# Spare bytes put the operands of all products at the same place modulo 512 bytes, and the software DMA scratch is halved

## The chip, the cores and the metric

The kernel runs on one core of one Trainium2 chip. Time is device time in microseconds (us) of one execution, the median of the runs shown; smaller is better. The engines are TensorE (PE, with its weight loads as PEld), VectorE (DVE), ScalarE (ACT), GpSimd (POOL) and SyncE (SP).

## The reference, cut to what matters

Two layers of a streaming encoder for 256 tokens of width 2048, all in float32. In each layer:

```
h = rms_norm(x, pre_mix_norm);  proj = h @ w_in                  # u, c_kv|k_pe, c_q, gate logits
a = mla(c_q, c_kv, k_pe) @ w_o                                   # 16 heads, chunk-causal mask
s = GLU(gelu(S5 scan of u) @ w_glu)
m = sigmoid(g_a) * a + sigmoid(g_b) * s
x = x + rms_norm(m @ w_out, post_mix_norm)
h = rms_norm(x, pre_ffn_norm)
x = x + rms_norm((silu(h @ w_gate) * (h @ w_up)) @ w_down, post_ffn_norm)
```

## The kernel before

All large products go through `gemm` (line 413). A weight matrix is taken in pieces of 256 rows by 512 columns. SP fetches a piece into a `raw` tile, ACT rounds it to float32r into a `hi` tile (line 187), and DVE subtracts the two into a `lo` tile (line 151, through the `Counted` wrapper). The activations lie split in the same way, feature by feature, as high and low parts. A product of 128 tokens, 128 features and 512 columns is then three matmuls, lines 444 to 446: high part with `hi`, high part with `lo`, low part with `hi`. In each of them the weights (`hi`, `lo`) are the moving operand, 512 columns of 4 bytes, so 2048 bytes of each partition, and the activations are the stationary operand, 128 columns of 4 bytes, so 512 bytes of each partition. A weight load (PEld) precedes each matmul, since the stationary operand alternates.

The stationary operand is, by stage: tile `H` for u, c_kv|k_pe, c_q, the gates, w_o and the gate and up products of the feed-forward; `uz` for w_glu; `mT` for w_out; `aT` for w_down. The c_kv|k_pe product alone has 320 columns in place of 512.

In the attention (lines 1293 to 1356) it is the other way round: the weight parts are stationary, and the activations `cqT` (lines 1306 to 1308) and `ckvT` (lines 1333 to 1335) move, 256 columns at a time; the values (lines 1351 to 1353) have the weights moving again. The S5 part has float32r products `bu` of `uz` with `bd` (lines 991 to 993). Transposes (line 467), scores, the products with the probabilities and `y` (line 1001) are plain float32. All these are set between or beside the large products by a planner in Python (`Background`), which fixes each engine's order when the program is built.

| tile | starts at | modulo 512 |
|---|---|---|
| `cs` (the identity among it) | 16512 | 128 |
| `raw`, `hi`, `lo` (15 tiles of 4096 bytes) | 17568 and on | 160 |
| `H` | 79008 | 160 |
| `X` (tokens by features, also the attention's arena) | 111776 | 160 |
| `uz`, and `aT` in its room later | 134880 | 224 |
| `mT` | 151264 | 224 |
| S5 tiles (`E`, `P`, `bd`, `xx`), layer 0, layer 1 | 163840 to 197120 | 0, 352 |
| `cqT`, layer 0, layer 1 | 203264, 202592 | 0, 352 |
| `ckvT`, `kpeT`, `pT`, layer 0, layer 1 | 198496 to 223743 | 0, 352 |

Inside a tile all the operands of 512 columns, 256 columns and 128 columns start at multiples of 512 bytes. The one exception is the second half of a weight piece in the 320-column product, which starts 1280 bytes into its tile, so at 416 modulo 512.

At the end of a mix or a feed-forward, `boundary` (line 669) adds the residual: POOL loads it in chunks `xo` and writes the new x (lines 684 and 690), DVE adds.

## Time and profile before

| | |
|---|---|
| median of 3 runs (lowest, highest) | 2937.29 us (2936.51, 2938.09) |
| span of the profiled execution | 2934.7 us |
| PE busy | 2902.1 us, 99% of the span |
| PEld, DVE, ACT busy | 80%, 65%, 48% |
| POOL busy | 33.1 us, 1% |
| HBM traffic | 188 GB/s over the span |

The span runs from the first to the last instruction; the profiled execution's time is not given apart, so 2937.29 - 2934.7 = 2.6 us are taken as lying around the span. PE's busy time is no measure of its pace, since matmuls overlap and their ends are modelled: two matmuls that start 227 ns apart both show some 390 ns. The pace is read from the starts.

### The profile page before, as it was taken

To read this page: it belongs to the slowest core of one execution; us is meant where nothing else is said; L and a number is where in the kernel's file an instruction comes from. 1 tells how busy PE (TensorE), PEld (TensorE's weight loads), DVE (VectorE), ACT (ScalarE), POOL (GpSimd) and SP (SyncE) were. 2 spreads that over 40 slices of the span, in tenths; PEclk is the share of its full clock that TensorE was granted. 3 is DMA by queue.
4 is the path that set the end of the run, shared out by engine and by line. 5 is a ranking of instruction groups with operands and counts; after the bars stand their busy time and mean duration, and the time that the engine had idled before them with its cause. 6 is when DMAs were issued, how large, how long until landed. Compare 5 with 4: busy or idle time off the path is not lost.

```text
span 2934.7 us, 37400 instructions
## 1 busy us (share of the span) xinstructions
PE 2902.1 (99%) x13557; PEld 2350.9 (80%) x13557; DVE 1902.7 (65%) x2988; ACT 1413.1 (48%) x2343; POOL 33.1 (1%) x65
## 2 busy tenths in 40 slices
PE   8999999999999999999999999999999999999998
PEld 7777887787788888888877778878878888888887
DVE  7888998765765554544478888986665554454444
ACT  6655665444544444333366556644445444444333
POOL 0000000000000000000000000000000000000000
PEclk9999999999999999999999999999999999999999
DMA  7666335666666666655576663357666566666554
GB/s 220 200 197 185 110 117 180 210 214 202 216 204 202 188 192 193 189 192 192 173 228 195 193 187 112 116 182 240 214 205 206 180 193 195 185 187 229 190 192 142
DMA packets 311222, 553.77 MB, mean 189 GB/s; under 512 B 44353, under 2 KB 57085, under 8 KB 310653
## 3 DMA queue, kind: packets, MB, share of 16 engines
q1 hardware_dynamic: 301708, 528.43, 57.8%
q0 software_dynamic: 4544, 14.42, 1.5%
q10 hardware_dynamic: 4784, 8.53, 0.8%
q8 instruction: 106, 1.74, 0.2%
q14 instruction: 80, 0.65, 0.1%
HBM read 532.74 MB, written 18.56 MB: 188 GB/s over the span
## 4 chain that ended last, share of the span: by engine, by line
PE 96%; DVE 2%; DMA 1%; ACT 0%; issue 0%; SPq 0%; DVEq 0%; ACTq 0%
PE acc L444 28%; PE acc L446 28%; PE acc L445 28%; PE y L1001 2%; PE aux L467 2%; PE bu L991 1%; PE acc L1306 1%; PE acc L1308 1%; PE acc L1307 1%; DVE lo L151 1%; PE bu L992 1%; PE bu L993 1%; PE aux L1286 0%; PE aux L1237 0%; PE aux L1238 0%
## 5 line engine op out<-in xcount | busy, mean ns | idle before, releaser
L151 DVE TENSOR_TENSOR lo<-raw,hi 128x1024 fp32r<-128x1024 f32 (+3 forms) x992 | 1147.8, 1172 | 620.9 <-PE acc L445 413.4
L187 ACT ACTIVATE hi<-raw 128x1024 fp32r<-128x1024 f32 (+3 forms) x992 | 994.1, 1018 | 748.6 <-PE acc L446 573.7
L444 PE MATMUL acc<-hi,H 128*128 128x512 f32 (+1 forms) x2432 | 963.7, 396 | 0.4 <-ACT X L264 0.3
L446 PE MATMUL acc<-hi,H 128*128 128x512 f32 (+1 forms) x2432 | 945.0, 389 | 4.6 <-DVE H L151 4.6
L445 PE MATMUL acc<-lo,H 128*128 128x512 f32 (+1 forms) x2432 | 944.4, 388 | 1.2 <-DVE lo L151 1.2
L444 PEld LDWEIGHTS acc<-hi,H 128*128 128x128 f32 x2432 | 457.2, 188 | 108.2 <-issue 13.2
L446 PEld LDWEIGHTS acc<-hi,H 128*128 128x128 f32 x2432 | 457.0, 188 | 103.5 <-DVE H L151 8.8
L445 PEld LDWEIGHTS acc<-lo,H 128*128 128x128 f32 x2432 | 457.7, 188 | 90.0 <-DVE lo L151 2.6
L444 PE MATMUL acc<-hi,aT 128*128 128x512 f32 x704 | 278.7, 396 | 0.0
L445 PE MATMUL acc<-lo,aT 128*128 128x512 f32 x704 | 278.4, 395 | 0.0
L446 PE MATMUL acc<-hi,aT 128*128 128x512 f32 x704 | 278.4, 395 | 0.0
L446 PEld LDWEIGHTS acc<-hi,aT 128*128 128x128 f32 x704 | 132.3, 188 | 32.0
L444 PEld LDWEIGHTS acc<-hi,aT 128*128 128x128 f32 x704 | 132.4, 188 | 31.8
L445 PEld LDWEIGHTS acc<-lo,aT 128*128 128x128 f32 x704 | 132.4, 188 | 31.8
L444 PE MATMUL acc<-hi,uz 128*128 128x512 f32 x256 | 102.4, 400 | 1.6 <-ACT uz L264 1.6
L444 PE MATMUL acc<-hi,mT 128*128 128x512 f32 x256 | 101.4, 396 | 0.0
L446 PE MATMUL acc<-hi,uz 128*128 128x512 f32 x256 | 101.2, 395 | 0.0
L445 PE MATMUL acc<-lo,uz 128*128 128x512 f32 x256 | 101.2, 395 | 0.0
L446 PE MATMUL acc<-hi,mT 128*128 128x512 f32 x256 | 100.9, 394 | 0.0
L445 PE MATMUL acc<-lo,mT 128*128 128x512 f32 x256 | 100.9, 394 | 0.0
L264 ACT ACTIVATE X<-acc,rstd 128x512 f32<-128x512 f32 (+1 forms) x64 | 41.2, 651 | 121.0 <-PE acc L446 119.4
L264 ACT ACTIVATE aT<-aux 128x512 fp32r<-128x512 f32 x44 | 26.1, 598 | 146.2 <-PE aux L467 146.2
(194 smaller groups left out, 2702.8 us busy)
## 6 DMA issues: line engine op xcount, KB each, us to landing
raw<-in_w_in_dram SPq DMA_DIRECT2D x176, 512.0 KB, 4.3
raw<-in_w_ffn_gate_dram SPq DMA_DIRECT2D x176, 512.0 KB, 4.2
raw<-in_w_ffn_up_dram SPq DMA_DIRECT2D x176, 512.0 KB, 3.8
raw<-in_w_ffn_down_dram SPq DMA_DIRECT2D x176, 512.0 KB, 4.4
raw<-in_w_o_mla_dram SPq DMA_DIRECT2D x64, 512.0 KB, 4.0
raw<-in_w_glu_dram SPq DMA_DIRECT2D x64, 512.0 KB, 4.9
raw<-in_w_out_dram SPq DMA_DIRECT2D x64, 512.0 KB, 4.7
raw<-in_w_uq_dram SPq DMA_DIRECT2D x32, 384.0 KB, 3.6
```

Source lines behind the costliest of these rows:

```text
L151: return f(**kw)
L187: self.nc.scalar.activation(out=dst(hv), in_=src(self.raw[n]), func=AF.Copy)
L264: ACT.activation(out=o, in_=x, func=f, **kw)
L444: PE.matmul(out=o, lhsT=xh, rhs=h[:, kk], start=(k == 0), stop=False)
L445: PE.matmul(out=o, lhsT=xh, rhs=lo[:, kk], start=False, stop=False)
L446: PE.matmul(out=o, lhsT=xl, rhs=h[:, kk], start=False, stop=(k == nk - 1))
L467: PE.transpose(o, x, ident[0:rows, 0:rows])
L991: PE.matmul(out=o, lhsT=bd[r, 0, i], rhs=uh, start=True, stop=False)
L992: PE.matmul(out=o, lhsT=bd[r, 1, i], rhs=uh, start=False, stop=False)
L993: PE.matmul(out=o, lhsT=bd[r, 0, i], rhs=ul, start=False, stop=True)
L1001: PE.matmul(out=yo, lhsT=cm[:, i, c].rearrange("p g q -> p (g q)"), rhs=xx[:, i], start=(i == 0), stop=(i == 1))
L1306: PE.matmul(out=o, lhsT=hi, rhs=cqT[:, 0, k], start=(k == 0), stop=False)
```

## The change

A helper `spare` takes a named tile that nothing reads or writes. It is called in three pools, so that what follows lies further up: 352 bytes behind `cs`, 448 bytes behind the tile `zero`, and 224 (layer 0) or 384 (layer 1) bytes at the head of the S5 pool. The scratch of the software DMAs goes from 16384 to 8192 bytes, which makes room for them. The rest of the diff blanks comments. On every engine the instructions, their order, their shapes and their waits are the same as before; only the addresses differ.

```diff
+    def spare(pool, n):
+
+        T(pool, [128, n // 4], "spare")
+
...
     cs = T(cp, [128, 262], "cs")
     ACT.dma_start(out=cs, in_=cst)
+    spare(cp, 352)
...
     zero = T(vp, [128, 1], "zero")
+    spare(vp, 448)
     V.memset(ap=zero, constant=0.0)
...
         def s5(l=l, gains=gains):
+            spare(sp, 224 if l == 0 else 384)
             tab = T(sp, [128, 928], "seeds")
...
-    nc = _bacc.Bacc("TRN2", target_bir_lowering=False, num_devices=1)
+    nc = _bacc.Bacc("TRN2", target_bir_lowering=False, num_devices=1, dynamic_dma_scratch_size=8192)
```

In the changed program `raw`, `hi`, `lo`, `H`, `X`, `uz`, `aT`, `mT`, `cqT`, `ckvT`, `kpeT`, `pT`, `bd` and `xx` all start at 0 modulo 512, in both layers. `cs` stays at 128, and the second half of a piece in the 320-column product lies at 256. `H` starts at byte 71168, `uz` and `aT` at 127488, `mT` at 143872.

## Rows read from the trace of the kernel before

**Rows 1.** The page: busy times, and the chain that ended last.

```profile
PE 2902.1 (99%) x13557; PEld 2350.9 (80%) x13557; DVE 1902.7 (65%) x2988; ACT 1413.1 (48%) x2343; POOL 33.1 (1%) x65
...
PE 96%; DVE 2%; DMA 1%; ACT 0%; issue 0%; SPq 0%; DVEq 0%; ACTq 0%
```

**Rows 2.** PE's groups by line and shape: count | busy us, mean ns | idle before.

```profile
L444 PE MATMUL acc<-hi,H 128*128 128x512 f32 x2368 | 943.2, 398 | 0.1
...
L444 PE MATMUL acc<-hi,aT 128*128 128x512 f32 x704 | 278.7, 396 | 0.0
...
L444 PE MATMUL acc<-hi,uz 128*128 128x512 f32 x256 | 102.4, 400 | 1.6 <-ACT uz L264 1.6
L444 PE MATMUL acc<-hi,mT 128*128 128x512 f32 x256 | 101.4, 396 | 0.0
...
L1306 PE MATMUL acc<-cqT,hi 128*128 128x256 f32 x192 | 58.0, 302 | 0.0
...
L991 PE MATMUL bu<-uz,bd 32*128 32x256 f32 x128 | 42.1, 329 | 0.0
...
L1333 PE MATMUL acc<-ckvT,hi 128*128 128x256 f32 x64 | 20.9, 326 | 0.0
...
L1351 PE MATMUL acc<-hi,ckvT 128*128 128x256 f32 x64 | 19.2, 300 | 0.0
```

**Rows 3.** Stretches with H, aT, mT, uz: length; busy us by engine; PEclk, DMA share.

```profile
975.00:1000.00 25.00, 25.00 (x112) 20.71 (x111) 13.16 (x12) 10.70 (x11) 0.00 (x0) 1.00 0.55 168
1230.00:1430.00 200.00, 200.00 (x859) 161.12 (x858) 91.93 (x82) 79.13 (x84) 0.00 (x0) 1.00 0.58 193
650.00:675.00 25.00, 25.00 (x109) 20.03 (x108) 11.24 (x11) 9.40 (x12) 0.00 (x0) 1.00 0.59 201
555.00:562.00 7.00, 7.00 (x31) 5.64 (x30) 6.30 (x8) 3.48 (x4) 0.00 (x0) 1.00 0.35 109
```

**Rows 4.** PE's timeline (start us, us): first and last matmul with H, and with aT.

```profile
974.66 0.39 PE L444 MATMUL acc<-hi,H 128*128 128x512 f32 x1
...
999.82 0.39 PE L444 MATMUL acc<-hi,H 128*128 128x512 f32 x1
...
1229.80 0.40 PE L446 MATMUL acc<-hi,aT 128*128 128x512 f32 x1
...
1429.99 0.40 PE L446 MATMUL acc<-hi,aT 128*128 128x512 f32 x1
```

**Rows 5.** PE's timeline, layer 0: y, then second and last of 24 q products.

```profile
343.31 1.05 PE L1001 MATMUL y<-xx,cm 128*32 128x256 f32 x4
...
344.51 0.28 PE L1307 MATMUL acc<-cqT,lo 128*128 128x256 f32 x1
...
347.14 0.29 PE L1308 MATMUL acc<-cqT,hi 128*128 128x256 f32 x1
```

**Rows 6.** Layer 1: y, then second, seventh and last of 24 q products.

```profile
1802.28 1.05 PE L1001 MATMUL y<-xx,cm 128*32 128x256 f32 x4 [0.40 <-DVE xx L151]
...
1811.94 0.28 PE L1307 MATMUL acc<-cqT,lo 128*128 128x256 f32 x1
...
1812.53 0.28 PE L1306 MATMUL acc<-cqT,hi 128*128 128x256 f32 x1
...
1814.46 0.28 PE L1308 MATMUL acc<-cqT,hi 128*128 128x256 f32 x1
```

**Rows 7.** PE's timeline, the 320-column product: first and last of 15.

```profile
61.78 0.31 PE L444 MATMUL acc<-hi,H 128*128 128x320 f32 x1
...
63.83 0.31 PE L446 MATMUL acc<-hi,H 128*128 128x320 f32 x1
```

**Rows 8.** DVE's groups, 60 to 420 us (layer 0), then 1530 to 1880 us (layer 1).

```profile
L151 DVE TENSOR_TENSOR P<-E,Z 128x512 f32<-128x512 f32 x47 | 31.4, 709 | 0.0
...
L151 DVE TENSOR_TENSOR P<-E,Z 128x512 f32<-128x512 f32 x52 | 34.6, 707 | 0.0
```

**Rows 9.** The chain of waits at the first boundary: start us, us, what.

```profile
727.32 5.78 DMA xo<-in_x_dram
```

## The prediction, made before the changed kernel ran

> **What bounds the kernel now.** I read the page first: PE is busy for 99% of the span, and the chain that ended last is 96% PE [rows 1]. PE's groups show next to no idle time before the large products, 0.0 to 1.6 us in a whole group [rows 2]. So no wait is left to remove. What can change is the pace at which PE goes through its matmuls, and that is all an address can touch here. The next view is therefore the start times.

> In a stretch with one stationary tile, the count of the stretch less one, over the time from its first to its last start, is the pace. With H: (999.82 - 974.66) / 111 = 226.7 ns. With aT: (1429.99 - 1229.80) / 858 = 233.3 ns. mT and uz are read from the counts of their stretches, which take in the matmul that reaches over the stretch's start: with a length of 0.39 us each, 25.00 us show (25.00 + 0.39) / 0.2267 = 112.0 at H's pace and 108.8 at aT's. H shows 112, mT 109. 7.00 us show 32 or 33 at H's pace and 31 or 32 at aT's; uz shows 31. So both go at aT's pace [rows 3, 4]. [...] Rows, columns and type are the same in all four. What differs is the place: with H moving and stationary operand both lie at 160 modulo 512, with the other three the moving one lies at 160 and the stationary one at 224.

> Layer 0 and layer 1 are a second pair, with the same code: the 24 q products have the moving cqT at 0 and at 352, the stationary weights at 160 in both. From the second to the last, 22 steps: 2.63 / 22 = 119.5 ns in layer 0 and 2.52 / 22 = 114.5 ns in layer 1, and its last 17 steps go at (1814.46 - 1812.53) / 17 = 113.5 ns [rows 5, 6]. So the place does act on float32r products, and by some 7 ns of each.

> **The change part by part.** No instruction is added, removed or moved, so each term is a count by a change of pace.

> *aT, uz, mT: from (160, 224) to (0, 0).* The lines 444, 445 and 446 have equal counts; with aT 3 x 704 = 2112 matmuls, with uz and with mT 3 x 256 = 768 each, in all 3648 [rows 2]. If what counts is that both operands lie at the same place, they take H's pace: 233.3 - 226.7 = 6.67 ns each (13.3 against 20.0 ns over the columns), so 3648 x 6.67 ns = 24.3 us less. All of it lies on PE, so on the path. Could something else become late there? At H's pace a stage already gets its weights: 12 matmuls eat a piece in 2.72 us, with DVE 13.2 of 25 us busy and ACT 10.7, and the DMA engines at a share of 0.55. With aT DVE is 91.9 of 200 us busy, ACT 79.1, the DMA share 0.58 [rows 3]. 3% more pace raises them by 3%. The cover stays.

> *H: from (160, 160) to (0, 0).* 3 x 2368 = 7104 matmuls of 512 columns [rows 2]. No row has two operands of such a product at 0. [...] I take no change, by the nearest row: in the 320-column product the moving operand lies at 160 for three matmuls and at 416 for the next three, with H at 160 in both, and the 15 go evenly, 2.05 / 14 = 146.4 ns or 13 ns over the 133.3 ns of the columns, as with H everywhere [rows 7]. A shift by 256 bytes does nothing, so a start on the 512-byte boundary is nothing special by itself, and the fine grid has to be below 256 bytes.

> [...]

> *256-column products: to (0, 0).* Each of these groups has three lines of equal count: q 3 x 192 = 576, half of them in each layer, keys 3 x 64, values 3 x 64, bu 3 x 128, in all 1344 [rows 2]. If the 13.3 ns of H hold for them too, they go at 106.7 + 13.3 = 120.0 ns. Layer 1's q then lose (120.0 - 114.5) x 288 = 1.6 us, layer 0's 0.1 us; the other 768 I leave where they are. The two paces seen, 113.5 and 119.5 ns, bound them: all at the one or all at the other moves 768 by at most 6 ns either way, 4.6 us, and with the q's a bound of 6 us either way. I take 1.7 us more.

> *Plain float32 products.* Four products of y take 1.05 us in layer 0 (xx at 0) and 1.05 us in layer 1 (xx at 352) [rows 5, 6]. They do not feel the place. I take nothing for them, nor for the scores and transposes, which have no such pair of rows.

> *DVE and ACT.* In S5 DVE's P<-E,Z took 709 ns with its tiles at 0 and 707 ns with them at 352 [rows 8]. raw, hi and lo keep their places to each other. Nothing. If it were something, PE would cover it in most stages, since DVE is busy for 65% [rows 1].

> *The halved scratch.* It concerns POOL's DMAs. POOL is busy for 33.1 us of the span in all [rows 1], so there are few of them. But the residual's load is on the chain at a boundary, 5.78 us [rows 9], so a delay there would count. I take nothing; if each of the loads that the chain waits for came one landing (5.78 us) later, three boundaries would cost 17 us.

> *The sum:* -24.3 + 1.7 = -22.6 us. From the span, 2934.7 - 22.6 = 2912.1, and with the 2.6 us around it 2914.7 us, against the median of 2937.29.

> **The rivals.**

> *The place is not the cause.* H lies in the lower part of the partition (from byte 79008), aT, uz and mT above 134880, and they stay up there. If the height makes the 6.67 ns, nothing changes: 2937. For it: in the large products height and place go together. Against it: cqT lies at 203264 and 202592 in the two layers, the same height, and its pace differs; and aT reaches over 90 KB without a change of pace over 200 us. [...]

> [...]

> *Slower: 0 is a bad place for H.* If the common place counts too and 0 costs what 224 does, H goes to 233.3 ns, +47.4 us, and the rest gains nothing: 2985. It decides from 22.6 us / 7104 = 3.2 ns per product with H; above that the gain is eaten. For it: the moving cqT at 0 is the slower of the two layers [rows 5, 6]. Against: there the stationary operand lies at 160, so that the two differ by 160, not by 0.

> *The scratch bites:* 2914.7 + 17 = 2932.

> **How the numbers follow.** A difference of 0.2%, 5.9 us, is about what a measurement can tell from no change. Forecast 66% (own range 2908 to 2922, from the 6 us of the 256-column products); place not the cause 10%; H gains too 12%, wholly or in part; H loses 10%; the scratch 2%. The range takes in the unchanged time above, and of the case in which H gains the part up to about half its gain: 2885 to 2939. Faster: 66 + 12 = 78%; same: 10 + 2 = 12%; slower: 10%.

> **What would show it.** The stretches with aT, uz and mT at 226.7 ns between starts, H's still at 226.7, the 320-column product at 146.7; q at 120 in both layers; P<-E,Z at 708 ns; the residual's loads landing in some 5 us as now. Wrong if aT stays at 233.3 ns (height), or if H's pace moves at all: 7104 matmuls make 7.1 us of each nanosecond.

## The result, and the profile after

The changed kernel takes 2914.05 us (median of 4 runs, 2913.07 to 2915.5) against 2937.11 us before (4 runs, 2936.51 to 2938.09): a ratio of 0.9921 with a 95% interval of 0.9907 to 0.9936. It is faster by 23.1 us, 0.8%. The forecast was 2914.7 us.

The page after: the span, PE's and the other engines' busy time, and the chain that ended last.

```profile
span 2913.7 us, 37400 instructions
...
PE 2882.4 (99%) x13557; PEld 2353.5 (81%) x13557; DVE 1902.1 (65%) x2988; ACT 1412.6 (48%) x2343; POOL 33.1 (1%) x65
...
PE 96%; DVE 2%; DMA 1%; ACT 1%; issue 0%; DVEq 0%; ACTq 0%
```

Against [rows 1] the counts are the same on every engine, PE is as full as it was and the chain is still 96% PE. DVE and ACT work as long as before. PE's idle time, span less busy, goes from 2934.7 - 2902.1 = 32.6 us to 2913.7 - 2882.4 = 31.3 us. So nearly all of the gain is not a wait: the same matmuls follow one another more closely. Of PE's waits the one for `bx` in S5 moved most, before and after (us in total, times, longest):

```profile
PE y L467 <- ACT bx L264: 1.6, 1, 1.6
...
PE y L472 <- ACT bx L268: 0.3, 1, 0.3
```

In the other profiled executions below this wait is between 0.0 and 2.1 us, wherever the tiles lie, so the change can't be credited with it.

Lines of the kernel stand 4 to 7 further down than before: 448 to 450 are the three products of `gemm`, 1313 to 1315 those of q.

The same four stretches as in [rows 3] (H, aT, mT, uz), 5 to 10 us earlier since the work ahead is done sooner: length; busy us of PE, PEld, DVE, ACT, POOL; clock, DMA share, GB/s.

```profile
965.00:990.00 25.00, 25.00 (x112) 20.72 (x111) 11.45 (x10) 10.98 (x12) 0.00 (x0) 1.00 0.65 197
1222.00:1422.00 200.00, 200.00 (x884) 165.66 (x883) 95.13 (x85) 81.58 (x87) 0.00 (x0) 1.00 0.61 200
645.00:670.00 25.00, 25.00 (x112) 20.69 (x111) 12.65 (x12) 10.01 (x13) 0.00 (x0) 1.00 0.62 212
549.00:556.00 7.00, 7.00 (x32) 5.77 (x32) 1.32 (x3) 1.99 (x3) 0.40 (x1) 1.00 0.52 168
```

H shows 112 matmuls in 25 us, as before. aT shows 884 in 200 us in place of 859, mT 112 in place of 109, uz 32 in place of 31. For uz 32 fits either pace in so short a stretch; what decides is the mean over its products that follow one another directly, 227.1 to 227.6 ns in the two layers where it was 233.3. The clock is 1.00 in both kernels, so it is not the clock. The weights keep up: DVE's share with aT goes from 91.9 to 95.1 us of 200, ACT's from 79.1 to 81.6.

PE's timeline (start us, us), the first and last matmul of the stretch with H and of the one with aT:

```profile
964.70 0.39 PE L449 MATMUL acc<-lo,H 128*128 128x512 f32 x1
...
989.86 0.39 PE L449 MATMUL acc<-lo,H 128*128 128x512 f32 x1
...
1221.78 0.39 PE L448 MATMUL acc<-hi,aT 128*128 128x512 f32 x1
...
1421.93 0.39 PE L449 MATMUL acc<-lo,aT 128*128 128x512 f32 x1
```

H: (989.86 - 964.70) / 111 = 226.7 ns, as in [rows 4]. aT: (1421.93 - 1221.78) / 883 = 226.7 ns, where [rows 4] had 233.3.

The q products after, second and last of 24, in layer 0 and then in layer 1, with a y product of layer 1 (lines 1313 to 1315 and 1008):

```profile
343.72 0.28 PE L1314 MATMUL acc<-cqT,lo 128*128 128x256 f32 x1
...
346.34 0.28 PE L1315 MATMUL acc<-cqT,hi 128*128 128x256 f32 x1
...
1786.70 0.28 PE L1314 MATMUL acc<-cqT,lo 128*128 128x256 f32 x1
...
1789.33 0.28 PE L1315 MATMUL acc<-cqT,hi 128*128 128x256 f32 x1
...
1791.81 1.05 PE L1008 MATMUL y<-xx,cm 128*32 128x256 f32 x4 [0.34 <-DVE xx L151]
```

Layer 0 goes at 2.62 / 22 = 119.1 ns, as it did [rows 5]. Layer 1 goes at 2.63 / 22 = 119.5 ns where it had 114.5 [rows 6]: it lost 5 ns a product. y is as it was.

The 320-column product in PE's timeline, first and last of 18:

```profile
60.52 0.30 PE L448 MATMUL acc<-hi,H 128*128 128x320 f32 x1
...
63.01 0.31 PE L450 MATMUL acc<-hi,H 128*128 128x320 f32 x1
```

DVE's groups in layer 1 (count | busy us, mean ns | idle before):

```profile
L151 DVE TENSOR_TENSOR P<-E,Z 128x512 f32<-128x512 f32 x50 | 33.3, 709 | 0.0
```

The residual's load on the chain at the first boundary (start us, us, what):

```profile
723.26 5.32 DMA xo<-in_x_dram
```

2.49 / 17 = 146.5 ns per product, 709 ns (706 in layer 0), 5.32 us: all three as before [rows 7 to 9].

**Where the 21.0 us of the span went.** I added up the distances from each matmul's start to the next one's, over both whole traces, by group (us):

| group | before | after | difference |
|---|---|---|---|
| aT | 492.9 | 478.9 | -14.0 |
| mT | 179.7 | 174.8 | -4.9 |
| uz | 182.3 | 178.5 | -3.9 |
| H, 512 columns | 1655.7 | 1657.2 | +1.6 |
| q | 72.8 | 73.8 | +1.1 |
| keys and values | 51.4 | 51.7 | +0.3 |
| transposes of X | 50.3 | 51.2 | +0.9 |
| transposes of `bx` | 5.2 | 3.8 | -1.4 |
| ahead of the first matmul | 5.8 | 5.4 | -0.5 |
| all of the span | 2934.7 | 2913.7 | -21.0 |

What is left, some 0.3 us, is spread over groups that each move by 0.2 us or less.

### The profile page after: what moved, and what is told of

Same layout as the page of the kernel before. It is cut to its first block, busy times and chain, and to the rows that moved or that the text cites. A ratio compares the mean times of both kernels' runs of the same rounds, so it can differ in the third digit from the quotient of the medians.

```text
span 2913.7 us, 37400 instructions
## 1 busy us (share of the span) xinstructions
PE 2882.4 (99%) x13557; PEld 2353.5 (81%) x13557; DVE 1902.1 (65%) x2988; ACT 1412.6 (48%) x2343; POOL 33.1 (1%) x65
## 4 chain that ended last, share of the span: by engine, by line
PE 96%; DVE 2%; DMA 1%; ACT 1%; issue 0%; DVEq 0%; ACTq 0%
PE acc L448 28%; PE acc L449 28%; PE acc L450 28%; PE y L1008 2%; PE aux L472 2%; PE bu L998 1%; PE acc L1313 1%; PE acc L1314 1%; PE acc L1315 1%; DVE lo L151 1%; DMA xo<-x 1%; PE bu L999 1%; DVE X L151 1%; PE bu L1000 1%; PE aux L1293 1%; PE aux L1244 0%
## 5 line engine op out<-in xcount | busy, mean ns | idle before, releaser
L448 PEld LDWEIGHTS acc<-hi,H 128*128 128x128 f32 x2432 | 457.5, 188 | 108.9 <-issue 13.2
L448 PE MATMUL acc<-hi,aT 128*128 128x512 f32 x704 | 274.4, 390 | 0.0
L450 PE MATMUL acc<-hi,aT 128*128 128x512 f32 x704 | 274.1, 389 | 0.0
L268 ACT ACTIVATE X<-acc,rstd 128x512 f32<-128x512 f32 (+1 forms) x64 | 41.2, 650 | 122.0 <-PE acc L450 119.5
L268 ACT ACTIVATE aT<-aux 128x512 fp32r<-128x512 f32 x44 | 26.1, 599 | 146.4 <-PE aux L472 146.4
```

What stands on the lines that cost most here:

```text
L268: ACT.activation(out=o, in_=x, func=f, **kw)
L448: PE.matmul(out=o, lhsT=xh, rhs=h[:, kk], start=(k == 0), stop=False)
L450: PE.matmul(out=o, lhsT=xl, rhs=h[:, kk], start=False, stop=(k == nk - 1))
```

## The experiments

In what follows, the distance is the byte at which the stationary operand of a product starts, less that of the moving one, modulo 256 (why 256 and not 512, the fourth experiment shows). A pace is the mean from start to start of products that follow one another directly. All paces are at a granted clock of 1.00.

### All operands at 160 in place of 0

```diff
     ACT.dma_start(out=cs, in_=cst)
-    spare(cp, 352)
```

> Like the changed kernel, but all operands lie at 160 modulo 512 in place of 0. Theory (what counts is the distance between the two operands, not where they lie): aT, uz and mT at 226.7 ns, H at 226.7, q at 119.4 in both layers, so the time of the changed kernel, 2914 us (2911 to 2917). Rival (the 512-byte boundary is needed for aT, uz and mT): they stay at 233.3 ns and the time is 2937 us.

Measured: 2913.95 us (median of 4, 2912.35 to 2918.51), ratio to before 0.992 (0.9904 to 0.9937). The stretches with aT and with mT:

```profile
1235.00:1435.00 200.00, 200.00 (x884) 165.61 (x883) 93.47 (x85) 80.31 (x85) 0.00 (x0) 1.00 0.57 196
...
650.00:675.00 25.00, 25.00 (x112) 20.69 (x111) 11.60 (x11) 11.00 (x16) 0.00 (x0) 1.00 0.58 198
```

884 and 112, as in the changed kernel; H goes at 227.7 ns over all its products in both kernels, q at 119.4 to 119.5. The boundary of 512 bytes is nothing; that the operands lie at one place is all of it.

### The halved scratch alone

```diff
-    nc = _bacc.Bacc("TRN2", target_bir_lowering=False, num_devices=1)
+    nc = _bacc.Bacc("TRN2", target_bir_lowering=False, num_devices=1, dynamic_dma_scratch_size=8192)
```

> The kernel before with the scratch of the software DMAs halved and no spare bytes: everything lies 8192 bytes lower, no place modulo 512 changes. Theory: aT, uz, mT stay at 233.3 ns and the time is that of before, 2937 us (within 3 us). Rival (the scratch, or the lower address of uz and aT, which now start below 131072, brought the gain): uz and aT at 226.7 ns, 2914 to 2918 us. Rival (a smaller scratch delays POOL's DMAs and was paid for out of the gain): above 2940 us, with the residual's loads landing later than in 5 to 6 us.

Measured: 2937.18 us (median of 10) against 2936.34 (13), ratio 1.000 (0.9991 to 1.0009). aT:

```profile
1235.00:1435.00 200.00, 200.00 (x859) 161.12 (x858) 90.85 (x81) 78.21 (x83) 0.00 (x0) 1.00 0.55 190
```

859, as before. The scratch costs nothing to halve. And since it moves everything down by 8192 bytes, a whole multiple of 512, the height in the partition does nothing either.

### Other distances in the kernel itself, first set

The changed kernel with the stationary tiles moved away, to another place in each layer: uz to 32 and 128, mT to 64 and 160, aT to 96 and 192 (the two numbers are layer 0 and layer 1), and the attention's tiles `cqT` and `ckvT` to 64 and 192. In the diff `mp` holds uz, `ap` the attention's tiles, `gp` mT and `fp` aT.

```diff
+            spare(mp, (32, 128)[l])
...
+            spare(ap, (64, 192)[l])
...
+            spare(gp, (64, 160)[l])
...
+            spare(fp, (96, 192)[l])
```

> The changed kernel with the stationary operand moved up from 0 by: uz 32 in layer 0, 128 in layer 1; mT 64, 160; aT 96, 192; moving weights and H stay at 0. In the attention the moving cqT is moved up by 64 in layer 0 and 192 in layer 1. Theory (the distance modulo 256 or less sets the cost): mT of layer 0 at 64 goes back to 233.3 ns, as in the kernel before, where the distance was the same 64; the other distances each have a pace of their own between 220 and 240 ns; q in layer 1 comes near 113.5 ns, its pace in layer 1 before, where the distance was 192 too. H stays at 226.7. Time between 2900 and 2945 us. Rival (only equality helps): all six stages at 233.3 ns, q at 119.4, 2938 us. Rival (the place of the stationary operand alone counts, 224 being a bad one): all six at 226.7 but for none, 2914 us.

Measured: 2932.49 us (one run). aT in layer 0 (distance 96) and layer 1 (192):

```profile
1235.00:1435.00 200.00, 200.00 (x855) 160.79 (x854) 91.19 (x82) 78.58 (x84) 0.00 (x0) 1.00 0.55 190
2700.00:2900.00 200.00, 200.00 (x875) 164.12 (x874) 92.66 (x84) 79.82 (x86) 0.00 (x0) 1.00 0.56 194
```

855 and 875 matmuls in 200 us: 234.3 and 228.9 ns. At 32, 64, 128 and 160 the paces are 233.3, 233.3, 233.0 and 233.4. So the gain is lost again by moving one operand by 32 bytes at the same height: this rules out the height for good. But 192 stands between the two levels, so "equal or not" is not the whole rule. H stays at 227.6 to 227.8 over both layers.

In the attention q and keys have the weights as the stationary operand, so `cqT` at 64 and 192 gives them the distances 192 (layer 0) and 64 (layer 1). The second and last of 24 q products in layer 0:

```profile
344.38 0.28 PE L1317 MATMUL acc<-cqT,lo 128*128 128x256 f32 x1
...
346.97 0.28 PE L1318 MATMUL acc<-cqT,hi 128*128 128x256 f32 x1
```

2.59 / 22 = 117.7 ns. Over all q products it is 117.4 ns at 192 and 115.0 ns at 64, against 119.3 to 119.4 at 0 in the changed kernel.

### Other distances in the kernel, second set

The same edit with uz at 224 and 320, mT at 256 and 384, aT at 288 and 448, the attention at 128 and 256.

> As the run before, with uz 224 in layer 0, 320 in layer 1; mT 256, 384; aT 288, 448; cqT 128, 256. Theory with a period of 256 bytes: mT of layer 0 (256) at 226.7 ns as at 0, since in the 320-column product a shift of the moving operand by 256 did nothing; aT of layer 0 (288) as uz at 32 in the run before, uz of layer 1 (320) as mT at 64, mT of layer 1 (384) as uz at 128, aT of layer 1 (448) as aT at 192; q in layer 1 (256) at 119.4. If the period is 128, 256 and 384 both give 226.7. Rival (only equality helps): all six at 233.3 ns, 2938 us. Rival (224 is a bad place of the stationary operand by itself): uz of layer 0 alone at 233.3.

Measured: 2933.42 us (one run). aT in layer 1 (448) and mT in layer 0 (256):

```profile
2700.00:2900.00 200.00, 200.00 (x875) 164.10 (x874) 93.23 (x83) 80.30 (x85) 0.00 (x0) 1.00 0.56 195
650.00:675.00 25.00, 25.00 (x112) 20.71 (x111) 10.91 (x10) 9.83 (x13) 0.00 (x0) 1.00 0.60 204
```

256 is as good as 0 (226.9 ns), 448 goes like 192 (228.9 both), 288 like 32 (233.3 both), 320 like 64 (233.3 both), 384 at 232.4 against 233.0 with 128. The period is 256 bytes. That also explains [rows 7]: 416 and 160 are 256 apart.

### Series of equal matmuls with the other engines idle

Behind the last instruction of the changed kernel, 42 series of 48 equal products each, with one of 96 ahead of them, whose results nothing uses; the text of the first of the distances:

```diff
+    for i in range(n): PE.matmul(out=o[0:128, 0:512], lhsT=st[:, 1:129], rhs=mv[:, 0:512], start=(i == 0), stop=(i == n - 1))
```

> The changed kernel, and behind its end 43 series of 48 equal matmuls each from two tiles of their own, nothing else running: moving operand at 0 modulo 512, stationary operand d bytes further. float32r with 512 columns and 128 stationary columns at d = 0, 4, 8, 16, 32 and on by 16 to 256; 64 and 32 stationary columns at d = 0 and 64; 256 columns at d = 0 to 240 by 16; bfloat16 at d = 0, 64, 96. Theory (the two reads of TensorE, moving operand and next stationary operand, meet in the memory, and their distance modulo 256 sets how often): the paces of the kernel come back with the other engines idle: 226.7 ns at 0 and 256, 233.3 at 64, 229.1 at 192; with 64 and 32 stationary columns the part over 213.3 ns falls to about a half and a quarter (at d = 64 from 20 to 10 and 5 ns), since fewer bytes are read; bfloat16, with half the bytes, at most half the excess. Rival (it is traffic of ACT, DVE or the DMAs that meets PE's reads): all float32r series at one pace, 214 to 216 ns. Rival (a fixed cost of float32r): 64 and 32 stationary columns as slow as 128. Some d that the kernel's tiles have not tried may lie below 226.7 ns; neither theory says which.

The window over all of the series, with the columns as above:

```profile
2932.00:3316.00 384.00, 384.00 (x2046) 305.67 (x2045) 0.00 (x0) 0.00 (x0) 0.00 (x0) 1.00 0.00 1
```

DVE, ACT and POOL do nothing and the DMA share is 0.00. PE's timeline gathers each series into a row, so the pace of a series is the next row's start less its own, over 48. Distances 0, 4 (lines 1498, 1499), 64, 80 (1504, 1505), 192, 208 (1512, 1513), 256 (1516); then 64 and 32 stationary columns at distance 0 (1517, 1518):

```profile
2940.36 11.05 PE L1498 MATMUL acc<-mv,st 128*128 128x512 f32 x48
2951.25 11.32 PE L1499 MATMUL acc<-mv,st 128*128 128x512 f32 x48
...
3007.06 11.35 PE L1504 MATMUL acc<-mv,st 128*128 128x512 f32 x48
3018.26 11.29 PE L1505 MATMUL acc<-mv,st 128*128 128x512 f32 x48
...
3096.45 11.15 PE L1512 MATMUL acc<-mv,st 128*128 128x512 f32 x48
3107.44 11.36 PE L1513 MATMUL acc<-mv,st 128*128 128x512 f32 x48
...
3140.73 11.04 PE L1516 MATMUL acc<-mv,st 128*128 128x512 f32 x48
3151.61 11.20 PE L1517 MATMUL acc<-mv,st 128*64 128x512 f32 x48
3162.65 11.28 PE L1518 MATMUL acc<-mv,st 128*32 128x512 f32 x48
```

10.89 / 48 = 226.9 ns at 0, 11.20 / 48 = 233.3 at 64, 10.99 / 48 = 229.0 at 192 and 10.88 / 48 = 226.7 at 256; the change of place at a series' start is in these. Without it (the last 24 steps of each series, ns):

| distance | 0 | 4 | 8 | 16 to 64 | 80 | 96 | 112 to 160 | 176 | 192 | 208, 224 | 240 | 256 |
|---|---|---|---|---|---|---|---|---|---|---|---|---|
| 512 columns | 226.7 | 232.5 | 230.7 | 233.3 | 231.9 | 234.4 | 233.3 | 230.0 | 228.9 | 233.3 | 226.7 | 226.7 |

The bare products repeat what the kernel showed at each distance that both have: 64 (233.3 and 233.3), 96 (234.4 and 234.3), 192 (228.9 and 228.9), 0 (226.7 both); only at 128 do they differ by more than 0.2 ns (233.3 here, 233.0 and 232.4 there). So the effect comes with PE's products alone: it needs no traffic of DVE, ACT or the DMAs.

No run shows the 213.3 ns of the expectation, the time of 512 columns by themselves. As an estimate it follows from the series: from 320 to 512 columns at distance 0 the pace grows by 226.7 - 146.7 = 80.0 ns (the 320 are in the next section), 0.417 ns a column, and 512 of them make 213.3. With fewer stationary columns the part over that should have shrunk with them; it did not: 230.0 ns with 64 and 231.7 with 32 of them at distance 0, 232.5 and 231.7 at distance 64. That expectation failed: the pace does not follow the number of stationary columns.

256 columns (distances 0 and 16, then 64 and 80), and bfloat16 with 512 columns at distances 0 and 64 (1537, 1538; a third series has 96):

```profile
3196.06 5.91 PE L1521 MATMUL acc<-mv,st 128*128 128x256 f32 x48
3201.80 5.85 PE L1522 MATMUL acc<-mv,st 128*128 128x256 f32 x48
...
3218.82 5.61 PE L1525 MATMUL acc<-mv,st 128*128 128x256 f32 x48
3224.26 5.86 PE L1526 MATMUL acc<-mv,st 128*128 128x256 f32 x48
...
3286.70 10.53 PE L1537 MATMUL acc<-mb,sb 128*128 128x512 bf16 x48
3297.07 10.52 PE L1538 MATMUL acc<-mb,sb 128*128 128x512 bf16 x48
```

With 256 columns 0 is among the worst, 5.74 / 48 = 119.6 ns (120.0 without the change of place), and 64 is the best, 5.44 / 48 = 113.3; 192 has 113.3 as well, 208 and 224 have 116.7, the others 117.8 to 120.0. That is the two layers of the kernel before: with cqT at 0 and the weights at 160 the distance is 160 (120.0 in the series, 119.7 over all of layer 0), with cqT at 352 it is 64 (113.3 in the series, 115.0 over all of layer 1). At 192 the two do not agree: 113.3 in the series, 117.4 for q in the first set of distances; no run says why. In bfloat16 the place does nothing: 215.8 ns in all three. In float32r no series of 512 columns here comes below 226.7 ns.

### Alternating places, other widths and steps

Another 31 series behind the changed kernel, again with one of 96 ahead of them. In four of them moving and stationary operand change place at every product. In the first two (distance 0/64): a product's own two operands at one place and the next product's weights 64 bytes off (line 1499); and the other way round, the next product's weights level with the operand that is moving (1500). Then the same with 128 bytes (1502, 1503). The others change the number of columns, the number of partitions and the step between elements. That a weight load runs beside the product before its own is seen in the changed kernel's trace: line 450's load starts at 965.39 us and takes 0.19, line 449's product starts at 965.38, line 450's own at 965.61.

```diff
+    for i in range(n): PE.matmul(out=o[0:128, 0:512], lhsT=st[:, 16 * (i % 2):16 * (i % 2) + 128], rhs=mv[:, 16 * (i % 2):16 * (i % 2) + 512], start=(i == 0), stop=(i == n - 1))
+    for i in range(n): PE.matmul(out=o[0:128, 0:512], lhsT=st[:, 16 * (1 - i % 2):16 * (1 - i % 2) + 128], rhs=mv[:, 16 * (i % 2):16 * (i % 2) + 512], start=(i == 0), stop=(i == n - 1))
...
+    for i in range(n): PE.matmul(out=o[0:128, 0:512], lhsT=st[:, 0:128], rhs=mv[:, 0:1024:2], start=(i == 0), stop=(i == n - 1))
```

> Again series of 48 float32r matmuls behind the end of the changed kernel. (1) Alternating places, 512 columns: (a) moving and stationary both at 0, then both at 64, and so on: the two operands of one matmul are level, but the weight load that runs beside it is 64 away from its moving operand; (b) moving at 0 with stationary at 64, then moving at 64 with stationary at 0: the reverse; (c) and (d) the same with 128. Theory (the next weights are read while this matmul moves, and those two reads meet): (b) 226.7 ns and (a) 233.3 ns. Rival (an operand pair of one matmul has to be level): (a) 226.7 and (b) 233.3. Rival (each read waits for its own turn after the read before it, whatever it is): neither at 226.7. (2) 128, 192, 320, 384, 448, 480 columns, stationary operand at 0 and 64. Theory of a fixed price for each matmul: the same 13.3 ns over the columns at 0 for 320 columns and more. If the price went with the bytes moved it would fall to 10 ns at 384. (3) distances 228 to 252 in steps of 4: 226.7 at 240 is known; no expectation which lies lower. (4) 64 of the 128 partitions at 0 and 64: 226.7 and 233.3 if the reads meet in each partition by itself. (5) moving or stationary operand with every second element, moving operand backwards or with its two halves interleaved: twice the bytes spanned; the meeting theory lets the pace change, a fixed cost leaves it at 226.7.

PE's timeline: the four alternating series with fixed 64 (1501) and fixed 128 (1504) behind each pair; 448 columns at 0 and at 64 (1513, 1514); moving every second element (1527):

```profile
2950.29 11.28 PE L1499 MATMUL acc<-mv,st 128*128 128x512 f32 x48
2961.40 11.27 PE L1500 MATMUL acc<-mv,st 128*128 128x512 f32 x48
2972.51 11.36 PE L1501 MATMUL acc<-mv,st 128*128 128x512 f32 x48
2983.71 11.13 PE L1502 MATMUL acc<-mv,st 128*128 128x512 f32 x48
2994.67 11.21 PE L1503 MATMUL acc<-mv,st 128*128 128x512 f32 x48
3005.72 11.30 PE L1504 MATMUL acc<-mv,st 128*128 128x512 f32 x48
...
3069.20 10.07 PE L1513 MATMUL acc<-mv,st 128*128 128x448 f32 x48
3079.11 9.86 PE L1514 MATMUL acc<-mv,st 128*128 128x448 f32 x48
3088.81 10.56 PE L1515 MATMUL acc<-mv,st 128*128 128x480 f32 x48
...
3221.04 21.82 PE L1527 MATMUL acc<-mv,st 128*128 128x512 f32 x48
3242.68 21.83 PE L1528 MATMUL acc<-mv,st 128*128 128x512 f32 x48
```

Neither alternation reaches 226.7 ns: 11.11 / 48 = 231.5 for both with 64 (fixed 64: 233.3), and 228.3 and 230.2 with 128 (fixed: 232.1). In the pair with 64 the distance that is not 0 goes between 64 and 192, whose fixed paces have the mean (233.3 + 228.9) / 2 = 231.1 ns: both alternations go as if the level pair brought nothing. Neither "a product's own two operands have to be level" nor "the next weights have to be level with what is moving" holds by itself. The third expectation on record, neither at 226.7 ns, is the one that came; what it gives as the cause no run shows. A fixed 128 took 233.3 ns in the series before and 232.1 here, the same text behind other products and on another chip; no run tells which of the two makes the difference. What makes the places differ stays open.

By columns, at distance 0 and 64, without the change of place (ns): 128: 111.7 and 111.7; 192: 111.7 and 111.7; 320: 146.7 and 146.7; 384: 173.3 and 176.7; 448: 206.7 and 202.2; 480: 216.7 and 215.9. Over the estimated 0.417 ns a column that makes 13.3 ns at distance 0 for 320, 384 and 512 columns, but 20.0 for 448 and 16.7 for 480: "13.3 ns for each product" is not a rule either, and a level place can lose (448 columns, by 4.5 ns, and 256, by up to 6.7).

Distances of 228, 232, 236, 244, 248 and 252 bytes took 230.7, 231.1, 231.7, 233.3, 233.3 and 226.7: none goes below 226.7. On 64 partitions it is 226.7 at distance 0 and 233.3 at 64, as on 128. With the stationary operand taking every second element, or the moving one going backwards, 233.3. With the moving one taking every second element, 21.64 / 48 = 450.8. The series meant to interleave the two halves of the moving operand reads its even elements first and then its odd ones, so with a step of two as well (last row); it took 451.1 ns.

### The attention at its own best distance

What the series say of 256 columns, put into the changed kernel: only the attention's tiles move, to 192, so that q and keys have distance 64 and the values 192.

```diff
+            spare(ap, (192, 192)[l])
```

> The changed kernel with 192 more spare bytes at the head of the attention's pool, so that cqT, ckvT and what follows lie at 192 modulo 512; all else as in the changed kernel. In the series 256 columns went at 113.3 ns with the stationary operand 64 or 192 bytes behind the moving one and at 120.0 ns level with it; in the kernel runs of 24 and 12 products reach less of it: q 115.0, keys 116.3, values 117.9 ns with cqT and ckvT at 192 against 119.4 level. Theory: 576 x 4.4 + 192 x 3.0 + 192 x 1.5 ns = 3.4 us less than the changed kernel, 2910.6 us, ratio to the kernel before 0.991. Rival (the products of the attention are not on the path): 2914 us, no change.

Measured: 2912.49 us (median of 5, 2911.46 to 2913.22), ratio to before 0.9912 (0.9899 to 0.9926). That is 1.6 us under the changed kernel's 2914.05, but the two were not run beside one another. So both ran again, side by side:

> The changed kernel once more, beside the next run on the same chip. Expected 2913.5 us (2912.5 to 2914.5). It leaves nothing out. If the distance of 192 bytes in the attention products is worth what the starts of single runs say, the next run is faster than this one by 3 us; if the difference of the medians so far (1.6 us) was that of two chips, by nothing.

> The changed kernel with the stationary operands of q, keys and values 192 bytes from the moving ones, beside the run before on the same chip. 264 products of 256 columns at 115.0 to 118.0 in place of 119.4 ns: 22 x 27 q, keys and values in all give 2.5 to 3.5 us, so 2910.5 us. Rival: the time won at these products is lost again at the groups behind them, and the two kernels are within 1 us of one another.

Measured: the changed kernel 2913.78 us (median of 5, 2913.41 to 2917.39), ratio to before 0.992 (0.9906 to 0.9934); with the attention at 192, 2912.07 us (median of 4, 2911.04 to 2914.23), ratio 0.9911 (0.9898 to 0.9925). The second and the last of 24 q products of layer 1, in the kernel with the attention at 192:

```profile
1770.11 0.28 PE L1317 MATMUL acc<-cqT,lo 128*128 128x256 f32 x1
...
1772.62 0.28 PE L1318 MATMUL acc<-cqT,hi 128*128 128x256 f32 x1
```

2.51 / 22 = 114.1 ns, where the changed kernel has 119.5. Over all q products 114.7 to 114.8 against 119.3 to 119.4, keys 117.4 to 117.7 against 119.3, values 117.3 against 119.3. By the starts this gives 2.5 us at q and 0.5 us at keys and values; the spans of the two profiled executions differ by 2912.0 - 2909.6 = 2.4 us, the medians by 1.7 us, and 17 of the 20 pairs of one run of each have the second kernel ahead. That these products go faster is shown by their starts. The gain in the median is at the edge of what these runs can tell, and smaller than was expected. In the two profiled executions other groups move by as much: the transposes of `bx` take 1.7 us more in the second kernel, the products with H 1.5 us less. The second kernel has the lowest median of those run.

## Why the prediction was right

**The bound.** PE's pace and not a wait: right. With 99% of the span busy before and after, PE's idle time moved by 1.3 us and the distance between starts made the rest.

**aT, uz, mT, forecast -24.3 us.** Right in mechanism, 1.5 us too much in size: -22.8. aT gave 14.0 us and mT 4.9, which is 2112 x 6.6 ns and 768 x 6.4 ns. uz gave 3.9 us, 5.1 ns a product: where its products follow one another directly they went from 233.3 ns to between 227.1 and 227.6, which makes 4.4 us, and the some 30 steps with a wait or another product between them took back half a microsecond. The weights did not become late: PE waits 1.1 us for `lo` and 0.3 us for `hi` in all, where it waited 1.2 us and nothing.

**H unchanged.** Right: 226.7 ns in an undisturbed stretch before and after, 227.6 to 227.8 over each layer in both. The +1.6 us of the table is 0.2 ns for each of 7104 products; it is of the size of the 1.5 us by which H differs between the last two kernels above, whose H lies at the same place. That H's shift of both operands together does nothing was tested directly by the kernel with all at 160. Its reading of the 320-column product, that a shift by 256 bytes does nothing, was right as well. That the grid then has to be finer than 256 bytes was not: the period is 256, since 128 goes at 232.4 to 233.3 ns.

**256 columns, forecast +1.7 us.** q went to 119.4 and 119.3 ns in the two layers where 120.0 was said, +1.1 us, and keys and values gave +0.3; bu, -0.1, stayed as it was. In all that is +1.3 us, so the term was right to 0.4 us. No run shows the terms of its ground, 106.7 ns for 256 columns (133.3 for 320) and 13.3 ns on top (20.0 for aT); what the runs show are whole paces, at distance 0 120.0 ns for 256 columns, 146.7 for 320 and 226.7 for 512. With the 0.417 ns a column that is estimated from the last two, the ground was only half right: 13.3 ns over the columns is what H pays, and 256 columns at distance 0 do pay it, but the series of 448 and 480 columns show that it is not the same for all.

**Plain float32, DVE, ACT, scratch: nothing.** Right: y 1.05 us as before, P<-E,Z at 706 and 709 ns, the first boundary's load 5.32 us, and the scratch by its own run 1.000 (0.9991 to 1.0009). Transposes with X rose by 0.9 us in all, which was not forecast; 0.5 us of it is PE's idle time before them (8.0 and 8.5 us), the rest is not explained.

**The sum.** -22.6 forecast, -21.0 in the profiled executions, 23.1 in the medians. The profiled execution of the changed kernel is the slowest of its four (2915.5 us), 1.5 us above the median. What lies around the span is 1.8 us in the run that was profiled (2915.5 - 2913.7), and not the 2.6 us that were taken. The terms that were forecast came to -22.8 + 1.3 = -21.5 us. What was not forecast adds up to +0.4 us only because H and the transposes of X on the one side, and the wait for `bx` and the earlier start on the other, nearly cancel. The mechanism and its two terms were right; that the median lies within 0.7 us of the forecast is luck, since the four runs alone are 2.4 us apart.

**The rivals.** That the height was the cause falls with the first set of distances: aT moved by 96 bytes at the same height and went to 234.3 ns. That H gains at the boundary, or loses at 0, falls with H's 226.7 at 0 and the equal time of the kernel at 160. No run shows a gain of H, which the lower end of the range, 2885 us, takes in. The scratch falls with its own run. What the prediction called the place was right as far as it went, but two things in it were too simple: it spoke of equal and unequal places, and the distances 176, 192 and 240 lie between or at the good level; and it gave no reason why layer 1's q were the faster ones, though their operands lie at unequal places: the series show that 256 columns have a distance of their own that is best for them.

## What to carry to other kernels

Where PE is full, read the distance between starts and compare it with an estimate of what the columns alone take (0.417 ns each at a granted clock of 1.00, from the 80.0 ns between 320 and 512 columns at distance 0); PE's busy share, 99% in both kernels, shows nothing of this. For float32r products of 512 columns put the stationary and the moving operand a multiple of 256 bytes apart (226.7 against 229 to 234 ns, 3%); for 256 columns 64 bytes past such a multiple (113.3 against 120.0 ns level in a bare series, 115 against 119.4 for q in the kernel; 192 is as good in the series, but q got only 117.4 from it), and for another width measure a series of 48 first, since there level can lose. This costs some spare bytes in a pool. For bfloat16 (215.8 ns at each of the three places tried) no run shows a use.

## What was not expected of the hardware

- The paces repeat after 256 bytes (226.7 ns at 0 and 256, 233.3 at 64 and 320), and the two directions are not alike: 4, 8 and 16 bytes one way cost 4 to 7 ns (232.5, 230.7 and 233.3 against 226.7), 4 and 16 bytes the other way (distances 252 and 240) cost nothing, 8 the other way (248) 6.7.
- float32r products of 128 and of 192 columns take the same 111.7 ns at either distance, about as much as 256 columns at their best place (113.3).
- A moving operand with a step of two elements takes 451 ns in place of 226.7, and so does one whose even elements are read first and then its odd ones; the stationary one with the same step takes 233.3.
- With DVE, ACT and POOL idle and the DMA share at 0.00 the distance alone moves the pace of float32r from 226.7 to 234.4 ns. Why it does is not settled by these runs.
